# Attention output projection by seven block products for six of its eight column blocks, with the modulation loads and decay constants moved a stage later

## The chip, the cores and the metric

The kernel runs on one core of a Trainium2 chip. The metric is the device time of one execution in microseconds, as the median of several runs. One profiled execution gives the trace; its times are in microseconds from the start of its span.

## The reference

One layer of a hybrid model: 640 tokens (128 of context, 512 latent) with 1024 channels go through an attention branch and a retention branch, whose outputs are projected, gated and added. Cut to what the change touches:

```
z = h @ w_in                                   # q, k, v, rq, rk, rv, rg, ga, gr are split from z
m = jax.nn.silu(cond) @ w_mod + b_mod          # split in 6: sh1, sc1, g1, sh2, sc2, g2
ya = attend_blocks(q, k_all, v_all)
yr, s_f, s_b = retention_branch(rq, rk, rv, rg, ret_pos, dec_f, dec_b, s0_f, s0_b)
y = jax.nn.sigmoid(ga) * (ya @ w_att_o) + jax.nn.sigmoid(gr) * (yr.astype(h.dtype) @ w_ret_o)
...
lg_f = jax.nn.log_sigmoid(dec_f.astype(jnp.float32))
```

The change is about `ya @ w_att_o`, a product of 640 x 1024 by 1024 x 1024, the w_mod products of sc2, sh2, g1 and g2, and the constants made from `dec_f` and `dec_b`.

## The kernel before

Every float32 factor is held as a rounded high part and a low part, and a product is three matmuls, high by high, high by low and low by high. The two halves of the 640 tokens (HALF is 320) are the moving side of a matmul of 128x320; a column block c of a weight is 128 of the 1024 output columns, and k runs over 8 blocks of 128 rows.

The projection is the stage of the PSUM pool `mm3` (five banks) and starts behind attention. `split` (L646/L647) makes high parts on ACT and low parts on DVE of the eight row blocks of the attention output `q4` (tiles `f0.s.3` and `f0.s.4` in the profile), into `ya.u1` and `ya.u2`. Then for each column block c, `load_w` brings two columns' weights and splits them (high part L145 on ACT, low part L150 on DVE, tiles `wh`), `b_col` (L195 to L197) issues 24 matmuls for each half, and `ya_ev` (L793) gates each bank on DVE with `tha[c]` (tiles `f1.s`); L795 spills it on POOL's queue. After each half step a generator, `mod_rest`, is advanced by one: it loads 2 MB of w_mod into a single buffer on SP's queue (L249), waits six steps, issues 64 small matmuls for it (L257) and some follow-up work (L260, L265). In this stage it does four loads (sc2, sh2). `decay_consts` (L580 to L601) makes the decay constants from two small loads; `decay_tables` (L813 to L817) uses them two groups later. A scheduler orders the instructions of each engine by the data they need.

Next come three groups, RK, RQ and RV, by `a_group` (L157 to L159, matmuls of 128x512); each runs in ten steps of twelve matmuls and loads two raw weight tiles of 1 MB. There `mod_rest` is advanced once a step and does the other four loads (g1, g2).

Much later the same kind of projection, `yr @ w_ret_o`, is done by a seven-product scheme (`ret_unit`). For two columns and both halves of the tokens, a pair p, the 2x2 block product is made from seven block products of four k blocks each, twelve matmuls, instead of eight. Its factors need sums: four sums of quarters of the activation (`ret_sums`, L1017 to L1029, each with a high part on ACT and a low part on DVE) and four sums of weight quarters for each pair (`wsum`, L1063). `prep` makes the two parts of one product's weights (L1073, L1082, or L1079 and L1080 through a DMA that accumulates). `prod` issues the matmuls (L1109, L1111, L1112) and the evictions: products 1, 6, 7, 4 add up in one bank and are copied out between (L1114, L1118, L1122, L1126), 5 and 3 share one (L1116, L1129), 2 has its own (L1120). The order of the products is 1, 5, 6, 2, 3, 7, 4, where 4 is held back by two places. A pump keeps up to eight `wh` tiles prepared. Under `tc.manual_schedule` PE, DVE and ACT issue in the order in which the code is written.

## Time and profile before

| what | value |
|---|---|
| median of 3 runs | 1179.63 us (1178.53 to 1179.68) |
| profiled execution | 1177.66 us |
| its span | 1175.9 us |
| mean granted TensorE clock | 0.996 |
| PE busy | 1146.9 us (98%) |
| DVE, ACT, POOL busy | 772.9, 589.7, 182.9 us |
| projection (262.4 to 328.3) | 65.9 us |

PE, DVE, ACT and POOL are TensorE, VectorE, ScalarE and GpSimd; PEld is the loading of weights into PE, and SP the queue that issues most loads. A row of a timeline gives start, duration, engine, line, operation, the tile that it writes and those that it reads, and in brackets how long the engine was idle before and for whom. In a windows row the columns are the stretch, its length, busy time and count for PE, PEld, DVE, ACT and POOL, the granted clock, the DMA share and GB/s.

### The profile page before, as it was taken

What the parts mean: (1) busy time and instruction counts of PE and PEld (TensorE: products, weight loads), DVE (VectorE), ACT (ScalarE), POOL (GpSimd) and SP (SyncE); (2) the same over time, 40 slices, a digit from 0 to 9 for tenths busy, and PEclk for the clock granted to TensorE, in tenths of its full rate; (3) what the DMA queues carried; (4) which work ended last, traced back from release to release, by engine and by line L of the source; (5) the groups of instructions that cost most, each with busy time, mean ns of one, the idle gap of its engine ahead of it and who ended that gap; (6) DMA issues with size and microseconds to landing.
All of it is one profiled execution on the core that took longest, in us unless ns stands there. A gap on an engine that the chain in (4) does not pass through costs nothing.

```text
span 1175.9 us, 18380 instructions
## 1 busy us (share of the span) xinstructions
PE 1146.9 (98%) x7269; PEld 1031.2 (88%) x7269; DVE 772.9 (66%) x1432; ACT 589.7 (50%) x1077; POOL 182.9 (16%) x194
## 2 busy tenths in 40 slices
PE   5999999999999999999999999999999999999995
PEld 4788899999988888888999988999899999899994
DVE  4566977665233536453847739969767588588887
ACT  4355656552132324442445526667657466565463
POOL 0042200000012100033002123002112111121013
PEclk9999999999999999999999999999999999999998
DMA  8742111115754521111117976435666656566553
GB/s 282 254 146 72 37 36 37 37 35 215 260 181 171 172 84 59 37 37 36 54 55 141 275 107 199 108 84 129 145 135 137 148 127 163 126 124 151 129 123 111
DMA packets 135878, 145.84 MB, mean 124 GB/s; under 512 B 26592, under 2 KB 101424, under 8 KB 135792
## 3 DMA queue, kind: packets, MB, share of 16 engines
q1 hardware_dynamic: 106880, 113.60, 29.9%
q0 software_dynamic: 28912, 31.07, 16.5%
q8 instruction: 57, 0.93, 0.3%
q14 instruction: 29, 0.24, 0.1%
HBM read 112.94 MB, written 8.65 MB: 103 GB/s over the span
## 4 chain that ended last, share of the span: by engine, by line
PE 90%; DVE 5%; ACT 2%; issue 1%; POOL 1%; DMA 0%; SPq 0%; DVEq 0%; ACTq 0%; POOLq 0%
POOL f0.s.5_3532 L950 0%; DMA xin.u1.1_108<-in_x_sample 0%; DVE gt.gt0.5_7309 L1380 0%; PE mm3.mm.72_6290 L1109 0%; DVE acts.u2.2_97 L415 0%; PE mm1.mm.11_300 L159 0%; PE mm7.mm.42_9455 L1553 0%; PE mm7.mm.30_8723 L1551 0%; PE mm7.mm.63_10822 L1551 0%; PE mm7.mm.54_10187 L1551 0%; PE mm7.mm.21_8240 L1551 0%; PE mm7.mm.57_10456 L1551 0%; PE mm7.mm.45_9704 L1551 0%; PE mm7.mm.42_9455 L1551 0%; PE mm7.mm.63_10822 L1554 0%
## 5 line engine op out<-in xcount | busy, mean ns | idle before, releaser
L795 POOL DMA_DIRECT2D spill.u2.2_2893<-f1.s.1_1165 x1 | 0.6, 586 | 130.1 <-DVE mod.u4.4_2852 L586 130.1
L1565 DVE TENSOR_TENSOR t7.u4.4_6978<-t7.u4.4_6978,const.u1.1_70 128x322 f32<-128x322 f32 x10 | 5.0, 496 | 11.8 <-ACT const.u1.1_70 L1564 11.8
L1080 POOL DMA_DIRECT2D weights.wh.164_5980<-weights.raw.156_5913 x1 | 1.3, 1347 | 69.5 <-DVE f1.s.9_5324 L1120 69.5
L888 DVE SCALAR_TENSOR_TENSOR ret2.u1.1_4329<-ret2.u1.1_4329,const.u13.13_93 64x128 f32<-64x128 f32 x24 | 6.8, 336 | 6.6 <-ACT ret2.u1.1_4329 L881 6.5
L890 DVE SCALAR_TENSOR_TENSOR ret2.u1.1_4329<-ret2.u1.1_4329,const.u13.13_93 64x128 f32<-64x128 f32 x24 | 6.6, 383 | 4.8 <-ACT ret2.u1.1_4329 L883 4.8
L841 DVE TENSOR_TENSOR ret.u5.5_3535<-ret.u5.5_3535,ret.u1.1_3528 128x512 f32<-128x512 f32 x5 | 3.5, 692 | 9.4 <-POOL ret.r2k.8_3713 L839 3.3
L1476 POOL TENSOR_TENSOR x1.u1.1_6484<-x1.u1.1_6484,weights.raw.422_11041 128x512 f32<-128x512 f32 x5 | 7.9, 1594 | 10.2 <-ACT x1.tm.112_11054 L1449 7.4
L841 DVE TENSOR_TENSOR ret.u4.4_3534<-ret.u4.4_3534,ret.u1.1_3528 128x512 f32<-128x512 f32 x5 | 3.5, 692 | 9.0 <-POOL ret.r2k.11_3893 L839 4.7
L565 POOL TENSOR_TENSOR p1.u1.1_609<-p1.u3.3_613,p1q.u1.1_603 128x512 f32<-128x512 f32 x1 | 1.3, 1307 | 44.8 <-DMA p1.u4.4_615<-in_cache_k 44.8
L150 DVE TENSOR_TENSOR weights.wh.108_4359<-weights.raw.106_4356,weights.wh.107_4358 128x1024 fp32r<-128x1024 f32 x1 | 1.2, 1225 | 10.3 <-ACT weights.wh.107_4358 L145 10.3
L412 ACT CAST acts.u1.1_96<-f0.s.2_110 128x640 fp32r<-128x640 f32 x4 | 2.9, 728 | 10.1 <-DVE f0.s.2_110 L410 10.1
L374 PE MATMUL mm1.mm.1_167<-const.u1.1_70,xin.u1.1_108 128*128 128x128 f32 x4 | 1.1, 435 | 7.0 <-DVE xin.u1.1_108 L365 7.0
L412 ACT CAST acts.u1.1_96<-f0.s.1_109 128x640 fp32r<-128x640 f32 x4 | 2.9, 726 | 9.8 <-DVE f0.s.1_109 L410 9.8
L145 ACT CAST weights.wh.112_4514<-weights.raw.111_4512 128x1024 fp32r<-128x1024 f32 x1 | 1.1, 1050 | 13.3 <-PE mm3.mm.36_4227 L158 13.3
L877 POOL DMA_DIRECT2D out_new_state_ret_fwd<-ret.r2k.25_4352 x1 | 0.7, 664 | 43.8 <-ACT ret.r2k.25_4352 L876 43.8
L260 DVE COPY mod2.wr.9_4319<-aux3.aux.15_4286 128x128 f32<-128x128 f32 x1 | 0.3, 290 | 10.9 <-PE aux3.aux.15_4286 L257 10.9
L950 POOL TENSOR_TENSOR f0.s.5_3532<-f0.s.5_3532,ret2.ny20.11_4911 128x512 f32<-128x512 f32 x5 | 6.0, 1237 | 9.1 <-DVE ret2.ny20.11_4911 L220 9.1
L534 ACT ACTIVATE f0.s.3_715<-f0.s.3_715,p1q.ny20.11_883 128x128 f32<-128x128 f32 x20 | 6.0, 388 | 2.5 <-DVE p1q.ny20.11_883 L218 2.5
L374 PEld LDWEIGHTS mm1.mm.1_167<-const.u1.1_70,xin.u1.1_108 128*128 128x128 f32 x4 | 0.7, 217 | 7.2 <-DVE xin.u1.1_108 L365 7.2
L145 ACT CAST weights.wh.67_3366<-weights.raw.66_3364 128x1024 fp32r<-128x1024 f32 x1 | 1.0, 1045 | 11.5 <-PE mm3.mm.8_3145 L196 11.5
L145 ACT CAST weights.wh.77_3621<-weights.raw.76_3619 128x1024 fp32r<-128x1024 f32 x1 | 1.0, 1045 | 11.5 <-PE mm3.mm.16_3458 L196 11.5
L145 ACT CAST weights.wh.72_3546<-weights.raw.71_3544 128x1024 fp32r<-128x1024 f32 x1 | 1.0, 1045 | 11.4 <-PE mm3.mm.12_3302 L196 11.4
(6929 smaller groups left out, 4936.2 us busy)
## 6 DMA issues: line engine op xcount, KB each, us to landing
spill.u1.1_2892<-x1.u1.1_6484 POOLq DMA_DIRECT2D x5, 512.0 KB, 3.9
xin.u1.1_108<-in_x_sample SPq DMA_DIRECT2D x4, 512.0 KB
p0.u5.5_125<-in_w_mod SPq DMA_DIRECT2D x2, 1024.0 KB
p0.u6.6_131<-in_w_mod SPq DMA_DIRECT2D x2, 1024.0 KB
p0.u7.7_134<-in_w_mod SPq DMA_DIRECT2D x2, 1024.0 KB
mod.wm.6_2920<-in_w_mod SPq DMA_DIRECT2D x1, 2048.0 KB
mod.wm.8_3073<-in_w_mod SPq DMA_DIRECT2D x1, 2048.0 KB
mod.wm.10_3230<-in_w_mod SPq DMA_DIRECT2D x1, 2048.0 KB
```

The costliest lines, as they stand in the source:

```text
L145: nc.scalar.copy(hi, rv)
L374: nc.tensor.transpose(xps[t, g][:, j * P:(j + 1) * P], xin[:, t, k * P:(k + 1) * P], ident)
L412: nc.scalar.copy(hT[0][:, k, :], xk)
L534: nc.scalar.activation(x[:, j], x[:, j], AF.Copy, scale=rstd[:, j:j + 1])
L565: nc.gpsimd.tensor_mul(ct, r2[:, :, 0, :], gqk[:, i:i + 1, :].to_broadcast([P, 4, P]))
L841: V.tensor_mul(z, z, r1[:, t, 0:1, :].to_broadcast([P, 8, 64]))
L888: V.scalar_tensor_tensor(Ss[0:64, hh, st + 1, j], Ss[0:64, hh, st, j], cdsel[0:64, h:h + 1], Ss[0:64, hh, st + 1, j], op0=ALU.mult, op1=AL ...
L890: V.scalar_tensor_tensor(Ss[64:128, hh, 2 - st, j], Ss[64:128, hh, 3 - st, j], cdsel[64:128, h:h + 1], Ss[64:128, hh, 2 - st, j], op0=ALU. ...
L950: nc.gpsimd.tensor_mul(ov, ov, rso[:, 4 * t:4 * t + 4].unsqueeze(2).to_broadcast([P, 4, P]))
L1080: nc.gpsimd.dma_start(lo, src, accum_op=ALU.add)
L1476: eng.tensor_mul(x, x, fg[:, c0:c0 + 512])
L1565: V.tensor_sub(u[1][:, hi_u], u[1][:, hi_u], u3[i])
```

## The change

The code of the seven-product scheme is taken out of `ret_unit` and made general (`seven_unit`, `seven_seq`, `seven_pump`, `seven_run`); w_ret_o uses it as it did. The attention projection now has three parts under a manual schedule. `two_cols` does columns 0 and 1 plainly, in four banks: k 0 to 3 of all four, then k 4 to 7, each bank gated at its end by `ya_ev` (L973 in the new file). `att_sums` and the lines behind it make the four sums in place in `q4` (L912, L916, L919, L923), with high parts by L905 and low parts by L908; they are advanced between the banks, ahead of the gates of those banks. Then pairs 1 to 3 (columns 2 to 7) go by seven products, whose casts are L804, low parts L813, weight sums L794, and whose copies out of banks are L826 (product 1), L828 (5), L830 (6), L834 (7) and L838 (4). The pump also prepares the first half of RK's weights. `decay_consts` and its loads move to the groups behind, into RQ's first step, and all eight w_mod loads are done there, with `mod_rest` advanced twice a step.

The core of the diff:

```
-    mp = Pool("mod", side="right")
-    dec = mp([P, 2, 8])
...
-    decay_consts(dec, dtmp)
-
-    ada = mod_rest((("sc", 1, 4096), ("sh", 1, 3072)), mp, aux)
+    lows, later = [], []
...
-    for c in range(KD):
-        if c % 2 == 0:
-            w = load_w(a["w_att_o"][0, :, c * P:(c + 2) * P], 8, 256)
-        cc = slice((c % 2) * P, (c % 2 + 1) * P)
-
-        def ya_ev(hf, ts, ps, c=c):
...
+    def att_sums():
+        s1, s3, s4 = qf[1, 1], qf[1, 0], qf[0, 1]
+        V.tensor_sub(s1, s1, qf[1, 0])
+        hi_sum(1, s1)
+        yield
+        lo_sum(1, s1)
+        V.scalar_tensor_tensor(s1, s1, -1.0, qf[0, 0], op0=ALU.mult, op1=ALU.subtract)
+        hi_sum(2, s1)
+        yield
+        V.tensor_sub(s3, qf[0, 0], s3)
+        hi_sum(3, s3)
+        lo_sum(2, s1)
+        yield
+        V.scalar_tensor_tensor(s4, s1, -1.0, s4, op0=ALU.mult, op1=ALU.subtract)
+        lo_sum(3, s3)
+        yield
+
+    def two_cols(w, act, ev):
+        banks = {}
+        for kh in range(2):
+            for c in range(2):
+                for hf in range(2):
+                    if kh == 0:
+                        banks[c, hf] = mm([P, 512], tag="mm")[:, :HALF]
+                    ps, ts = banks[c, hf], slice(hf * HALF, (hf + 1) * HALF)
+                    for k in range(4 * kh, 4 * kh + 4):
...
+                    yield
+                    if kh:
+                        ev(c, hf, ts, ps)
...
+    units = {p: seven_unit(w_ao[:, 2 * p * P:2 * (p + 1) * P], ar, u_of(p), p == 1, att_fin(p)) for p in range(1, KD // 2)}
+    seq = seven_seq(units)
+    pump = seven_pump(units, seq, [lambda: wrk.append(w_raw(w_in[:512, O_RK:O_RK + 512], 4, 512))],
+                      [(2, lambda h=h: wrk.append(w_split(wrk[0][:, 1024 * h:1024 * (h + 1)], 2, 512))) for h in range(2)])
+    with tc.manual_schedule(engines={ET.PE, ET.DVE, ET.Activation}):
+        def ya_ev(c, hf, ts, ps):
             V.scalar_tensor_tensor(tha[c][:, ts], tha[c][:, ts], 1.0, ps, op0=ALU.add, op1=ALU.mult)
             if hf:
                 nc.gpsimd.dma_start(thd[:, c, :], tha[c])
-        for _ in b_col(w, cc, yaTk, mm, ya_ev):
-            next(ada, None)
-    run(ada)
-    mp.close()
+
+        for n, _ in enumerate(two_cols(w, yaTk, ya_ev)):
+            if n in (0, 1, 3):
+                next(sums)
+            elif n == 2:
+                pump(-1, 1)
+            elif n == 4:
+                pump(-1, 2)
+            elif n == 5:
+                next(sums)
+            elif n == 6:
+                pump(-1, 4)
+        hi_sum(4, qf[0, 1])
+        lo_sum(4, qf[0, 1])
+        ut.append(f0())
+        seven_run(units, seq, pump)
+        wrk.append(load_w(w_in[512:, O_RK:O_RK + 512], 4, 512))
...
-    ada = mod_rest((("g", 0, 2048), ("g", 1, 5120)), mp, aux)
+    dec = mp([P, 2, 8])
+    dtmp = [mp([P, 2, 8]) for _ in range(3)]
...
+    ada = mod_rest((("sc", 1, 4096), ("sh", 1, 3072), ("g", 0, 2048), ("g", 1, 5120)), mp, aux)
...
-        for j, _ in enumerate(a_group(w_in[:, off:off + 512], hTk, mm, ev)):
+        first = None if i else (lambda: [x + y for x, y in zip(*wrk[1:3])], lambda: wrk[3])
+        for j, _ in enumerate(a_group(w_in[:, off:off + 512], hTk, mm, ev, first=first)):
+            if i == 1 and j == 0:
+                decay_consts(dec, dtmp)
+            next(ada, None)
             next(ada, None)
```

The core of the general unit, which is that of `ret_unit` with the factors and the final step passed in:

```
+        def prep(m):
+            if m in (5, 6):
+                low_part()
+            if m in (4, 5, 6):
+                wsum(m)
...
+            nc.scalar.copy(hi, src)
+            ops[m] = (hi, lo)
+            if m == 5:
+                wsum(7)
+            low_part()
+            if m in (2, 3) and not early:
+                nc.scalar.activation(lo, src, AF.Copy, scale=-1.0)
+                nc.gpsimd.dma_start(lo, src, accum_op=ALU.add)
+            else:
+                lows.append(lambda: V.tensor_sub(lo, src, hi.bitcast(F32)))
...
+            if m == 1:
+                nc.scalar.copy(u[0][:, los], ps)
+            elif m == 5:
+                nc.scalar.activation(u[1][:, his], ps, AF.Copy, scale=-1.0)
+            elif m == 6:
+                nc.scalar.activation(u[1][:, los], ps, AF.Copy, scale=-1.0)
```

What stands on DVE at the start of the projection, before (`ya.u2` are the low parts of the activation, `mod` tiles belong to the decay constants, `wh.60` is a weight's low part, `mm3.mm.1` the first bank):

```order
L647 TENSOR_TENSOR ya.u2.2_2829<-f0.s.3_715,ya.u1.1_2828 128x640 x3
L580 TENSOR_SCALAR mod.u2.2_2850<-mod.u1.1_2849 128x16
L647 TENSOR_TENSOR ya.u2.2_2829<-f0.s.3_715,ya.u1.1_2828 128x640
L647 TENSOR_TENSOR ya.u2.2_2829<-f0.s.4_964,ya.u1.1_2828 128x640 x4
L581 TENSOR_TENSOR mod.u2.2_2850<-mod.u2.2_2850,mod.u1.1_2849 128x16
L593 TENSOR_SCALAR const.u11.11_91<-mod.u1.1_2849 128x16
L150 TENSOR_TENSOR weights.wh.60_3057<-weights.raw.56_3050,weights.wh.59_3056 128x1024
L583 TENSOR_SCALAR mod.u3.3_2851<-mod.u2.2_2850 128x16
L793 SCALAR_TENSOR_TENSOR f1.s.1_1165<-f1.s.1_1165,mm3.mm.1_2904 128x320
```

And under the change, at the same place (`ysum` tiles are the parts of the sums, `raw.56` the raw weights of pair 1, `wh.57` and `wh.58` its first two prepared tiles):

```order
L647 TENSOR_TENSOR ya.u2.2_2829<-f0.s.3_715,ya.u1.1_2828 128x640 x4
L647 TENSOR_TENSOR ya.u2.2_2829<-f0.s.4_964,ya.u1.1_2828 128x640 x4
L912 TENSOR_TENSOR f0.s.4_964<-f0.s.4_964,f0.s.3_715 128x4x320
L908 TENSOR_TENSOR ysum.u2.2_2854<-f0.s.4_964,ysum.u1.1_2853 128x1280
L916 SCALAR_TENSOR_TENSOR f0.s.4_964<-f0.s.4_964,f0.s.3_715 128x4x320
L813 TENSOR_TENSOR weights.wh.57_2917<-weights.raw.56_2915,weights.wh.57_2917 128x512
L919 TENSOR_TENSOR f0.s.3_715<-f0.s.3_715 128x4x320
L908 TENSOR_TENSOR ysum.u4.4_2856<-f0.s.4_964,ysum.u3.3_2855 128x1280
L794 TENSOR_TENSOR weights.raw.56_2915<-weights.raw.56_2915 128x4x128 x2
L813 TENSOR_TENSOR weights.wh.58_2949<-weights.raw.56_2915,weights.wh.58_2949 128x512
L973 SCALAR_TENSOR_TENSOR f1.s.1_1165<-f1.s.1_1165,mm3.mm.1_2871 128x320
L923 SCALAR_TENSOR_TENSOR f0.s.4_964<-f0.s.4_964 128x4x320
```

The decay work is gone from between the low parts; behind the last low part three of the four sums, two of their low parts, two weight sums and two weight low parts now stand ahead of the first gate, and before it was one weight's low part and three small operations.

On ACT, behind the first casts of the activation, before (`wh.59`, `wh.62` and `wh.64` are high parts of weights):

```order
L646 CAST ya.u1.1_2828<-f0.s.3_715 128x640
L646 CAST ya.u1.1_2828<-f0.s.4_964 128x640 x4
L145 CAST weights.wh.59_3056<-weights.raw.56_3050 128x1024
L582 ACTIVATE mod.u2.2_2850<-mod.u2.2_2850 128x16
L145 CAST weights.wh.62_3209<-weights.raw.61_3207 128x1024
L597 ACTIVATE const.u13.13_93<-const.u12.12_92 128x8
```

And under the change (`mm3.mm.5` is the bank of product 1 of pair 1, `wh.57` to `wh.60` the weights of its products 1, 5, 6 and 2):

```order
L646 CAST ya.u1.1_2828<-f0.s.4_964 128x640 x4
L905 CAST ysum.u1.1_2853<-f0.s.4_964 128x1280
L905 CAST ysum.u3.3_2855<-f0.s.4_964 128x1280
L804 CAST weights.wh.57_2917<-weights.raw.56_2915 128x512
L905 CAST ysum.u5.5_2857<-f0.s.3_715 128x1280
L804 CAST weights.wh.58_2949<-weights.raw.56_2915 128x512
L804 CAST weights.wh.59_2983<-weights.raw.56_2915 128x512
L804 CAST weights.wh.60_2985<-weights.raw.56_2915 128x512
L905 CAST ya.u1.1_2828<-f0.s.4_964 128x4x320
L826 COPY f0.s.5_3006<-mm3.mm.5_3007 128x320
```

Four casts of sums and four of weights now stand in one row behind the activation's casts, and the first copy of a product's bank stands behind all eight.

More of the change, by code (lines that the diff above doesn't have):

```diff
@@ L773, in hybrid_step, with low_part @@
     yaTk = [[x[:, k] for k in range(KD)] for x in yaT]
[L774 to L781 removed]
+    lows, later = [], []
+    def low_part():
+        while lows:
+            lows.pop(0)()
@@ new lines, in seven_run @@
+    def seven_run(units, seq, pump, between=None):
+        pend = []
+        for n, (p, m) in enumerate(seq):
+            units[p][2](m)
+            pend.extend((n + d, fn) for d, fn in later)
+            later.clear()
+            if between:
+                between(n)
+            pump(n + 1, min(5 + n, 8))
+            for x in [x for x in pend if x[0] <= n]:
+                x[1]()
+                pend.remove(x)
+        for _, fn in sorted(pend, key=lambda x: x[0]):
+            fn()
@@ L1092, in reload, with tl_load @@
+    def tl_load(n):
+        if n == 15:
             for f in range(2):
                 tl.append(f1())
[L1094 to L1129 removed]
@@ L1131, in ret_unit @@
-        return load, prep, prod, reload
-    w_out = a["w_out"][0]
-    later, pend, wo0 = [], [], []
-    units = [ret_unit(p) for p in range(KD // 2)]
-    order = (1, 5, 6, 2, 3, 7, 4)
-    seq, held = [], []
-    for p in range(KD // 2):
-        for m in order[:-1]:
-            seq.append((p, m))
-            held = [(n - 1, y) for n, y in held]
-            if held and held[0][0] == 0:
-                seq.append(held.pop(0)[1])
-        held.append((2, (p, 4)))
-    seq += [y for _, y in held]
@@ L1146, in hybrid_step @@
[L1146 to L1165 removed]
+                nc.sync.dma_start(tl[f], thd[:, KD - 2 + f, :])
@@ L1167, in hybrid_step @@
+    ar = {1: ya[0, 0], 2: ya[0, 1], 4: ya[1, 1], 3: ys[4]}
+    units = {}
+    seq = seven_seq(range(KD // 2))
     wg = load_w(w_in[:, O_GR:O_GR + 2 * P], 8, 256)
```

252 lines of the change are left out of this document (138 added, 114 removed).

## The prediction

> **What bounds the kernel now.** I read the page's busy times first, then the windows around the stage that changes, then the PE timeline and the chain of waits inside it, and last the DVE and ACT timelines of places where the same operations run today. The page's engine row:
>
> ```profile
> PE 1146.9 (98%) x7269; PEld 1031.2 (88%) x7269; DVE 772.9 (66%) x1432; ACT 589.7 (50%) x1077; POOL 182.9 (16%) x194
> ```
>
> PE is busy 98% of a span of 1175.9 us (the profiled execution took 1177.66 us, 1.97 below the median of 1179.63). The windows view gives the stage before's projection fills and the one after it; the columns are length, busy time of PE, PEld, DVE, ACT and POOL with counts, granted clock, DMA share, GB/s:
>
> ```profile
> 262.40:328.30 65.90, 65.90 (x651) 64.10 (x650) 28.84 (x73) 13.35 (x20) 3.85 (x7) 1.00 0.63 228
> 328.30:430.00 101.70, 101.70 (x619) 82.76 (x622) 39.03 (x72) 29.02 (x52) 17.59 (x21) 1.00 0.47 160
> ```
>
> PE is busy 65.90 of 65.90 us in the projection, and 101.70 of 101.70 behind it, while DVE has 28.84 and ACT 13.35 us of work there. So a matmul removed is its full time gained, and any wait that PE gets is its full time lost. How little PE loses today is seen at the start of the stage, in its timeline:
>
> ```profile
> 262.75 0.31 PE L195 MATMUL mm3.mm.3_2962<-ya.u1.1_2828,weights.wh.52_2896 128*128 128x320 f32 x1
> 263.03 0.41 PE L196 MATMUL mm3.mm.1_2904<-ya.u2.2_2829,weights.wh.52_2896 128*128 128x320 f32 x1
> ```
>
> Before's scheduler puts matmuls of three banks in turn, so that the first correction (L196), which needs the first low half, starts 0.28 us after the matmul ahead of it. That 0.13 us beyond the pitch (0.147, next) is all I see lost there.
>
> **What is removed.** The matmul count falls from 8 columns x 2 halves x 8 k x 3 = 384 to 96 for two plain columns and 3 x 7 x 12 = 252 for six columns by seven products: 36 fewer. The pitch comes from the w_ret_o stage, which runs the same products with the same shape; its first two products on the PE timeline, twelve matmuls apart:
>
> ```profile
> 613.15 0.31 PE L1109 MATMUL mm3.mm.63_5899<-yr.u1.1_5318,weights.wh.152_5832 128*128 128x320 f32 x1
> ...
> 614.91 0.31 PE L1109 MATMUL mm3.mm.64_5921<-f0.s.7_5528,weights.wh.153_5836 128*128 128x320 f32 x1
> ```
>
> 1.76 us for twelve is 0.1467 us each, and 36 of them are **-5.28 us**. The Trainium skill, page "TensorE: Matmul & The Clock Gate", section "Back-to-back issue gap", gives N/2.4 GHz plus about 2.5 ns for a warm matmul, which would be 135.8 ns for 320 columns and 4.89 us for the 36; the rows here show 146.7, so the trace decides, and the difference is 0.39 us. In w_ret_o the scheme costs PE almost nothing beside its matmuls, as the waits of PE there show (total, times, longest):
>
> ```profile
> PE mm3.mm.66_6024 L1109 <- ACT f1.s.12_5327 L1118: 0.2, 1, 0.2
> ```
>
> One wait of 0.2 us in 28 products. That speaks for the change. But there the sums of the activation were made stages earlier, under other matmuls, and weights were prepared four tiles ahead. Here the activation is ready only as the stage begins, and PE has 96 plain matmuls, 14.1 us, to cover all preparation.
>
> **What is added ahead of the products.** For the sums the rows are those of w_ret_o's own sums, DVE and then ACT, 128x1280:
>
> ```profile
> 592.37 1.49 DVE L1023 TENSOR_TENSOR rt.u1.1_5323<-rt.u1.1_5323,yr.u2.2_5319 128x1280 f32<-128x1280 f32 x1
> 595.25 1.49 DVE L1029 TENSOR_TENSOR yr.u2.2_5319<-rt.u1.1_5323,yr.u1.1_5318 128x1280 fp32r<-128x1280 f32 x1 [1.38 <-ACT yr.u1.1_5318 L1028]
> ```
>
> ```profile
> 593.96 1.26 ACT L1028 CAST yr.u1.1_5318<-rt.u1.1_5323 128x1280 fp32r<-128x1280 f32 x1 [1.28 <-DVE rt.u1.1_5323 L1023]
> ```
>
> A sum or a low part is 1.49 us of DVE, a high part 1.26 us of ACT, and a low part begins 0.03 to 0.06 us behind its high part (593.96 + 1.26 = 595.22, then 595.25). Preparing a weight tile (128x512), on DVE a low part (L1082) and a sum (L1063), on ACT negation, cast and eviction in a row:
>
> ```profile
> 621.50 0.69 DVE L1082 TENSOR_TENSOR weights.wh.162_5958<-weights.raw.156_5913,weights.wh.162_5958 128x512 fp32r<-128x512 f32 x1
> 622.22 0.69 DVE L1063 TENSOR_TENSOR weights.raw.156_5913<-weights.raw.156_5913 128x512 f32<-128x512 f32 x1
> ```
>
> ```profile
> 625.09 0.63 ACT L1079 ACTIVATE weights.wh.165_5984<-weights.raw.156_5913 128x512 fp32r<-128x512 f32 x1
> 625.63 0.60 ACT L1073 CAST weights.wh.166_6001<-weights.raw.156_5913 128x512 fp32r<-128x512 f32 x1
> 626.13 0.42 ACT L1122 COPY f1.s.9_5324<-mm3.mm.63_5899 128x320 f32<-128x320 f32 x1
> ```
>
> 0.69 us each on DVE, 0.62 us on ACT (0.52 from start to start when queued), 0.42 for an eviction. A plain column's gate on DVE is the row of before's own eviction:
>
> ```profile
> 269.50 0.48 DVE L793 SCALAR_TENSOR_TENSOR f1.s.1_1165<-f1.s.1_1165,mm3.mm.1_2904 128x320 f32<-128x320 f32 x1
> ```
>
> Twelve sum operations are four sums and four low parts on DVE, 8 x 1.49 = 11.9 us, and four casts on ACT, 5.0 us. They can't start before the low halves of the activation, the last work of DVE that the stage opens with:
>
> ```profile
> 262.15 2.29 DVE L647 TENSOR_TENSOR ya.u2.2_2829<-f0.s.3_715,ya.u1.1_2828 128x640 fp32r<-128x640 f32 x3
> ...
> 264.44 0.82 DVE L647 TENSOR_TENSOR ya.u2.2_2829<-f0.s.3_715,ya.u1.1_2828 128x640 fp32r<-128x640 f32 x1
> 265.18 3.02 DVE L647 TENSOR_TENSOR ya.u2.2_2829<-f0.s.4_964,ya.u1.1_2828 128x640 fp32r<-128x640 f32 x4
> ```
>
> The eighth low half ends at 265.18 + 3.02 = 268.20.
>
> **The walk.** Under the change PE, DVE and ACT go strictly in the written order, so I walked the three queues by hand with these durations, each operation starting when its queue and its inputs allow (0.03 us behind the same engine, 0.06 us over from another, 0.10 to PE). On before's time axis:
>
> a) The first bank now takes k 0 to 3 at once, with nothing of another bank between. The fourth low half ends at 264.44 + 0.82 = 265.26, so its twelve matmuls, which could end at 264.21, end at 265.70: **1.49** late. The other seven groups and product 1 of pair 1 follow without a wait to 279.79.
>
> b) DVE: sum 1 at 268.3, its cast on ACT to 271.1, its low part to 272.7, sum 2 to 274.2, then a wait for ACT (cast of sum 2, then cast of weight tile 1) to 276.1, low part of tile 1, sum 3 and low part 2 to 279.7, two weight sums and a low part to 281.7, and only then the gate of the first plain bank, to 282.2. Product 5 needs that bank (five banks, four of them plain, one product 1's). It starts at 282.27 instead of 279.79: **2.48**.
>
> c) DVE next has sum 4, low part 3 and a second gate, and the weight sum of product 6 ends at 286.0. ACT waits for this sum with the cast of tile 6, then casts tile 2 and the high part of sum 4 (1.26), and behind these stands the copy of product 1 out of its bank, 288.3 to 288.8. Product 6 adds into that bank, so it starts at 288.86 and not at 284.03: **4.83**. This is the largest term: a copy that could run at 280 stands behind a queue that waits for DVE.
>
> d) Later a bank's copy stands behind weight casts that wait for their DVE sums: product 4 of pair 1 waits 1.32 (copy of 7), product 6 of pair 2 0.68 (copy of 1), product 7 of pair 2 0.54 (copy of 6): **2.54**. A last wait of 0.75 ahead of the final product lies behind three RK matmuls that the order puts there, and costs nothing.
>
> The waits are 1.49 + 2.48 + 4.83 + 2.54 = 11.34 us. Their bounds: with every hand-over free the walk gives 10.2, with 0.12 us for each 12.5; if the 1280-wide operations take 0.75 of their rows, 7.8. For d) zero (as in w_ret_o) to twice as much.
>
> **What is moved.** All eight w_mod loads of 2 MB now run under RK, RQ and RV, twice as often. The 64 matmuls of each load, and the issue of each load on SP's queue (L249):
>
> ```profile
> L257 PE MATMUL aux3.aux.9_3665<-mod2.wm.2_3569,mod2.s128.1_3566 x64: 272/273/297, 347.8 to 349.5; 128*32 128x128 f32 x64
> ...
> L257 PE MATMUL aux3.aux.11_3835<-mod2.wm.4_3736,mod2.s128.1_3566 x64: 272/273/297, 372.3 to 374.0; 128*32 128x128 f32 x64
> ```
>
> ```profile
> L249 SPq DMA_DIRECT2D mod2.wm.2_3569<-in_w_mod x1: 1068/1068/1068, 326.7 to 326.7; - x1
> L249 SPq DMA_DIRECT2D mod2.wm.4_3736<-in_w_mod x1: 367/367/367, 349.8 to 349.8; - x1
> ```
>
> Two sets start 24.5 us apart, of which 1.88 are the set itself, so a load has half of 22.6, **11.3 us**, from the release of its only buffer to its next set. When loads landed is read from the transfer rate by windows:
>
> ```profile
> 338.00:339.00 1.00, 1.00 (x6) 0.82 (x5) 0.00 (x0) 0.00 (x0) 0.00 (x0) 1.00 0.60 225
> 339.00:340.00 1.00, 1.00 (x6) 0.83 (x5) 0.00 (x0) 0.00 (x0) 0.00 (x0) 1.00 0.14 53
> 357.00:358.00 1.00, 1.00 (x6) 0.83 (x5) 0.31 (x1) 0.76 (x1) 0.66 (x1) 1.00 0.05 16
> ```
>
> The one issued at 349.8 had landed by 357.1 (7.3 us); the one at 326.7, beside the rope table and a 1-MB weight load, by 339.3 (12.6 us). The SP queue keeps the weight loads between, and before's projection ran 228 GB/s without a PE wait, while the stage behind it (160 GB/s over 101.7 us, 16.3 MB) rises by 8.4 MB over 7.5 us more, to some 226. I take 0.3 us in all, for the first load, and keep 0 and 1.3 per load as ends. The decay constants are small operations off PE's path and needed only by the tables in RV; their two loads stand on SP ahead of the first w_mod load. I put them at nothing: DVE and ACT have 60% idle there. The RK weights' first half is prepared under the products; nothing of it is late in the walk.
>
> **The sum.** -5.28 + 11.34 - 0.13 (before's own loss) + 0.3 = **+6.23**, own time 1177.66 + 6.23 = 1183.89, and beside a median that lay 1.97 higher, 1185.9.
>
> **The rivals.** Differences under 0.2%, 2.4 us, can't be told from no change by this measurement. The forecast has a chance of 0.60.
>
> *The later waits don't come* (0.15). PE, once late, gives DVE and ACT time, and w_ret_o showed one wait only; against it, the same queues here start without four tiles in hand. Waits 8.80: +3.69, median 1183.3.
>
> *The clock falls in the 4.8 us pause* (0.10 as a case of its own). The windows at the end, after the last matmul at 1164.02:
>
> ```profile
> 1164.00:1167.00 3.00, 0.02 (x1) 0.00 (x0) 2.86 (x13) 2.53 (x8) 0.53 (x1) 1.00 0.01 3
> 1167.00:1168.00 1.00, 0.00 (x0) 0.00 (x0) 0.96 (x4) 1.00 (x3) 0.54 (x1) 0.82 0.39 150
> 1168.00:1169.00 1.00, 0.00 (x0) 0.00 (x0) 0.96 (x3) 1.00 (x2) 0.00 (x0) 0.50 1.02 385
> ```
>
> A clock of 0.82 in the second of these means that full rate ended near 1167.64, after 3.6 us of no matmul. At the kernel's start, after 6.98 us idle, groups of four transposes:
>
> ```profile
> 13.13 1.12 PE L374 MATMUL mm1.mm.1_167<-const.u1.1_70,xin.u1.1_108 128*128 128x128 f32 x4 [6.98 <-DVE xin.u1.1_108 L365]
> ...
> 17.40 0.60 PE L374 MATMUL mm1.mm.6_213<-const.u1.1_70,xin.u1.1_108 128*128 128x128 f32 x4
> 17.84 0.60 PE L374 MATMUL mm1.mm.7_225<-const.u1.1_70,xin.u1.1_108 128*128 128x128 f32 x4
> ```
>
> Five groups took 4.27 us where one takes 0.44 later: 2.07 us lost. In the walk product 6 at half rate just uses up the waits of d), and the end stays where it was. Without these waits it adds to the rival above: +5.8. With both it is +8.3, median 1187.9. The Trainium skill, the page named above, section "What's actually happening", puts the fall to 1.2 GHz at an idle window of about 3.4 us; the trace's 3.6 agrees.
>
> *Each w_mod load comes late* (0.09). For it: 12.6 us in one case against 11.3. Against: 7.3 in the other. 1.3 x 8 = 10.4 at most, half of it the likely size: +11.1, median 1190.8.
>
> *The sums are cheaper than their rows, and the change wins* (0.06). In place it is one mechanism: the 1280-wide operations of c) and b). At half their price the walk's first two waits in b) and c) shrink to 0.17, all waits to 4.1, and with d) gone too to 1.66: -3.45, median 1176.2. Against it: every row of such an operation shows 1.49, in place or not. It decides the sign when all waits are under 5.1 us, and is a gain that can be told when they are under 2.7. Total waits between 2.7 and 7.5 would be no difference.
>
> **Range and chances.** The range takes in the walk at 0.75 of the sums' price (waits 7.8, +2.7, median 1182.3) with half of d) gone (1181.0), and on the other side d) doubled with the clock's 2.07 (+10.8, 1190.5). I give 1181.0 to 1190.5. Faster by over 0.2%: 0.05, most of the last rival. Within: 0.07, the rest of it and the low end of the first. Slower: 0.88.
>
> **What would show it.** In the profile after: PE's waits in the stage on L973 (about 2.5 us, product 5) and L826 (about 4.8, product 6), a first bank stretched by 1.5 us, small ones on L826, L830 and L834; granted clock below 1.00 behind the long wait; DVE's 1280-wide rows at 1.49; sets of L257 some 13.1 us apart from 335 on without waits on DMA. I am wrong if PE stays full through the stage, if the copy of product 1 (L826) comes near 280, or if the lost time is found behind the stage.

## The result and the profile after

The change makes the kernel slower: 1185.45 us (1185.35 to 1186.38, 4 runs) against 1179.08 us before (4 runs), a ratio of 1.0056 with a 95% interval of 1.0044 to 1.0068. That is 6.4 us. The profiled execution of the changed kernel has a span of 1183.8 us, 7.9 above that of before; 1.0 of this lies ahead of the stage, in the start of the kernel, which no edit touches. From the first matmul of the projection to the first product of the w_ret_o stage it is 357.14 us (263.48 to 620.62 on the PE timeline) against 350.70 (262.45 to 613.15): 6.44 us more, the same as the medians say.

The page's engine row: PE has 36 instructions fewer and is 97% busy in place of 98%, and DVE 24.7 us more.

```profile
PE 1146.4 (97%) x7233; PEld 1027.2 (87%) x7233; DVE 797.6 (67%) x1464; ACT 607.1 (51%) x1115; POOL 188.5 (16%) x198
```

The longest waits of PE in the projection and the three groups behind it; before's list of waits was empty for the projection (total, times, longest):

```profile
PE mm3.mm.5_3007 L821 <- ACT f0.s.5_3006 L826: 4.4, 1, 4.4
PE mm3.mm.6_3029 L821 <- DVE f1.s.1_1165 L973: 2.0, 1, 2.0
PE aux3.aux.10_4011 L265 <- DVE mod2.wr.15_3980 L260: 0.3, 1, 0.3
PE mm3.mm.8_3132 L821 <- ACT f0.s.5_3006 L826: 0.3, 1, 0.3
PE aux3.aux.1_3473 L257 <- DMA mod2.wm.6_3435<-in_w_mod: 0.3, 1, 0.3
```

The two large ones are those at product 6 of pair 1, for L826, and at product 5, for L973. The PE timeline has both, and how long product 6 took (first rows of products 5, 6 and 2):

```profile
282.88 0.39 PE L821 MATMUL mm3.mm.6_3029<-ysum.u1.1_2853,weights.wh.58_2949 128*128 128x320 f32 x1 [1.99 <-DVE f1.s.1_1165 L973]
...
289.25 0.63 PE L821 MATMUL mm3.mm.5_3007<-ysum.u3.3_2855,weights.wh.59_2983 128*128 128x320 f32 x1 [4.37 <-ACT f0.s.5_3006 L826]
...
292.42 0.31 PE L821 MATMUL mm3.mm.7_3074<-ya.u1.1_2828,weights.wh.60_2985 128*128 128x320 f32 x1
```

Product 6 starts 6.37 us behind product 5, where its turn would be 1.76, and itself takes 292.42 - 289.25 = 3.17 us and not 1.76. The granted clock says why, in the column ahead of DMA share and GB/s:

```profile
288.00:289.00 1.00, 0.00 (x0) 0.00 (x0) 1.00 (x3) 1.00 (x2) 0.00 (x0) 0.89 0.21 82
289.00:290.00 1.00, 0.76 (x3) 0.76 (x4) 1.00 (x2) 1.00 (x3) 0.39 (x1) 0.50 0.00 0
...
292.00:293.00 1.00, 1.00 (x8) 1.00 (x7) 0.52 (x1) 0.45 (x1) 0.00 (x0) 0.91 0.03 10
```

It fell in the pause, at about 288.8, and was at half rate until 292.2. Behind that PE hardly waits: 0.47 us at product 6 of pair 2 and 0.36 at product 7, from start to start. What ACT did ahead of product 6's release, and DVE ahead of that:

```profile
286.57 0.62 ACT L804 CAST weights.wh.59_2983<-weights.raw.56_2915 128x512 fp32r<-128x512 f32 x1 [4.96 <-DVE weights.raw.56_2915 L794]
287.10 0.61 ACT L804 CAST weights.wh.60_2985<-weights.raw.56_2915 128x512 fp32r<-128x512 f32 x1
287.62 1.25 ACT L905 CAST ya.u1.1_2828<-f0.s.4_964 128x1280 fp32r<-128x1280 f32 x1
288.78 0.41 ACT L826 COPY f0.s.5_3006<-mm3.mm.5_3007 128x320 f32<-128x320 f32 x1
```

```profile
282.65 1.48 DVE L923 SCALAR_TENSOR_TENSOR f0.s.4_964<-f0.s.4_964 128x1280 f32<-128x1280 f32 x1
284.05 1.49 DVE L908 TENSOR_TENSOR ysum.u6.6_2858<-f0.s.3_715,ysum.u5.5_2857 128x1280 fp32r<-128x1280 f32 x1
285.46 0.48 DVE L973 SCALAR_TENSOR_TENSOR f1.s.1_1165<-f1.s.1_1165,mm3.mm.2_2886 128x320 f32<-128x320 f32 x1
285.85 0.69 DVE L794 TENSOR_TENSOR weights.raw.56_2915<-weights.raw.56_2915 128x512 f32<-128x512 f32 x1
```

ACT waited 4.96 us for the weight sum of product 6 (L794, 285.85), which stands on DVE behind sum 4 (L923), low part 3 (L908) and a gate (L973); then come two casts, the high part of sum 4 and only then the copy. This is the chain of the prediction's point c), step by step: once the 1.03 us by which the stage starts later are taken off, each step comes 0.1 to 0.6 us ahead of where the walk has it.

### The profile page after: what moved, and what is told of

It reads as the page before. It is cut to its first block, busy times and chain, and to the rows that moved or that the text cites. A ratio compares the mean times of both kernels' runs of the same rounds, so it can differ in the third digit from the quotient of the medians.

```text
span 1183.8 us, 18404 instructions
## 1 busy us (share of the span) xinstructions
PE 1146.4 (97%) x7233; PEld 1027.2 (87%) x7233; DVE 797.6 (67%) x1464; ACT 607.1 (51%) x1115; POOL 188.5 (16%) x198
## 4 chain that ended last, share of the span: by engine, by line
PE 57%; DVE 4%; ACT 3%; issue 2%; DMA 1%; POOL 1%; DVEq 0%; ACTq 0%; POOLq 0%; SPq 0%
DMA weights.wh.419_10834<-weights.raw.406_10564 0%; DMA weights.raw.423_10893<-in_w_down 0%; POOL f0.s.6_3402 L1152 0%; DVE gt.gt0.5_7362 L1489 0%; PE mm3.mm.69_6341 L821 0%; PE mm7.mm.42_9508 L1660 0%; PE mm7.mm.30_8776 L1660 0%; PE mm7.mm.54_10240 L1660 0%; PE mm7.mm.33_9025 L1660 0%; PE mm7.mm.45_9757 L1660 0%; PE mm7.mm.21_8293 L1660 0%; PE mm7.mm.57_10509 L1660 0%; PE mm7.mm.54_10240 L1663 0%; PE mm7.mm.30_8776 L1663 0%; PE mm7.mm.39_9376 L1660 0%
## 5 line engine op out<-in xcount | busy, mean ns | idle before, releaser
L260 DVE COPY mod2.wr.21_4372<-aux3.aux.15_4339 128x128 f32<-128x128 f32 x1 | 0.3, 292 | 10.9 <-PE aux3.aux.15_4339 L257 10.9
L1552 DVE TENSOR_TENSOR x1.u1.1_6537<-x1.u1.1_6537,gate.u1.1_6508 128x512 f32<-128x512 f32 x10 | 6.8, 688 | 0.0
L1009 ACT ACTIVATE ret.u2.2_3400<-const.u1.1_70,const.u11.11_91 128x128 f32<-128x128 f32 x8 | 3.1, 388 | 7.1 <-DVE const.u11.11_91 L594 7.1
```

The costliest lines, as they stand in the source:

```text
L1009: nc.scalar.activation(dmat[:, h, :], cst[:, C_RF:C_RF + P], AF.Exp, scale=lg[:, 0, h:h + 1])
L1552: V.tensor_mul(x1[:, t, gs], x1[:, t, gs], gb[:, t == 0, gs])
```

## The experiments

The measure beside the time is the stage's length, from the first matmul of the projection to the first of the last product, from the PE timeline. It has 336 matmuls at 0.1467 and 0.70 us of three RK matmuls, 49.99 us without a wait. In the change it is 324.09 - 263.48 = 60.61. The first four runs shared a chip, then the next three, then the last three, each with runs of the kernel before.

**The moves alone.** The kernel before with the w_mod loads and the decay constants moved:

```
-        for _ in b_col(w, cc, yaTk, mm, ya_ev):
-            next(ada, None)
-    run(ada)
+        run(b_col(w, cc, yaTk, mm, ya_ev))
...
+            if i == 1 and j == 0:
+                decay_consts(dec, dtmp)
+            next(ada, None)
             next(ada, None)
```

> The kernel before, with only the moves of the change: all eight w_mod loads and the decay constants under RK, RQ and RV, the projection as it was. Theory A (the loss is made by the waits of the projection's products, the moves cost little): the trace of the change shows two pauses of about 0.5 us at the moved sets, so about 1180 us, within 0.2% of the kernel before. Theory B (the moves are the price, through loads that land late): 1183 us or more, with PE waiting for w_mod loads several times.

Measured: 1180.37 us, ratio 1.001 (1.0001 to 1.0018). From the projection's first matmul to w_ret_o it is 351.76 us, 1.06 more than before. PE waits twice behind the stage:

```profile
PE aux3.aux.11_4012 L257 <- DMA mod2.wm.16_3949<-in_w_mod: 0.4, 1, 0.4
PE aux3.aux.10_3951 L265 <- DVE mod2.wr.15_3920 L260: 0.3, 1, 0.3
```

So the moves cost about 1.1 us, one late load and one wait for the copy of a finished set (L260); no load is late again and again. The other 5.3 of the 6.4 us are the products.

**Without the sums.** The activation's sums and their parts are left out, and products 5, 6, 7 and 3 use plain quarters:

```
-    ysum = {m: [ysp([P, 4, HALF], F32R) for _ in range(2)] for m in (1, 2, 3)}
-    ysum[4] = yq[1, 0]
+    ysum = {1: yq[1, 1], 2: yq[0, 0], 3: yq[0, 1], 4: yq[1, 0]}
...
-        hi_sum(4, qf[0, 1])
-        lo_sum(4, qf[0, 1])
```

> The change without the four sums of the activation and their high and low parts: the products that need a sum take a plain quarter instead, so the output is not the reference's. Theory A (the sums fill DVE and ACT and hold PE up): the pauses of product 5 and product 6 go, about 1.5 us at the first bank and about 1 us later remain, so -5.3 + 2.0 + 1.0 - 0.1 = -2.4 against the kernel before, about 1176.7 us, and no fall of the clock. Rival (weight preparation alone is too slow for the products): pauses of 2 us and more remain, and the time is 1180 us or more.

Measured: 1176.58 us, ratio 0.998 (0.9972 to 0.9989), within 0.2 us of what theory A gave. The stage is 51.95 us long. The longest wait of PE in it:

```profile
PE mm3.mm.1_2862 L936 <- DVE ya.u2.2_2829 L647: 0.3, 1, 0.3
```

The weights alone keep up with PE; the pauses belong to the sums, and without them the seven products win 2.6 us.

**Copies and gates first.**

```
-                    yield
                     if kh:
                         ev(c, hf, ts, ps)
+                    yield
...
             elif n == 5:
+                pump(-1, 4)
+            elif n == 6:
                 next(sums)
-            elif n == 6:
-                pump(-1, 4)
-        hi_sum(4, qf[0, 1])
-        lo_sum(4, qf[0, 1])
+        def sum4(n):
+            if n == 0:
+                hi_sum(4, qf[0, 1])
+                lo_sum(4, qf[0, 1])
```

> The change with the evictions put ahead: each gate ahead of the sums and weights of its step, the preparation of products 6 and 2 ahead of the fourth sum, and that sum's parts behind the copy of product 1. Nothing is left out. Theory A1 (the prediction's words: copies stand behind sums in the queue, and this place is the price): the pause of product 6 falls from 4.4 us to about 1, so 1180.5 to 1182.5 us. Theory A2 (DVE and ACT have a fixed row of work with hand-overs up to product 7 of pair 2, and PE must wait for its end wherever the copies stand): pauses only move to products 3, 7 and 4 of pair 1, and the time stays within 0.8 us of the change, 1184.7 to 1186.2 us.

Measured: 1188.24 us, ratio 1.0075 (1.0062 to 1.0089), and a stage of 62.03 us, 1.42 longer than the change's. Both theories missed: the pause of product 6 did not fall. The waits of PE, then the two rows of DVE and ACT that end it:

```profile
PE mm3.mm.5_3005 L821 <- ACT f0.s.5_3004 L826: 5.0, 1, 5.0
PE mm3.mm.6_3029 L821 <- ACT weights.wh.58_2950 L804: 1.2, 1, 1.2
```

```profile
287.71 1.48 DVE L908 TENSOR_TENSOR ysum.u6.6_2858<-f0.s.3_715,ysum.u5.5_2857 128x1280 fp32r<-128x1280 f32 x1
```

```profile
289.31 0.42 ACT L826 COPY f0.s.5_3004<-mm3.mm.5_3005 128x320 f32<-128x320 f32 x1 [4.12 <-DVE ysum.u6.6_2858 L908]
```

The copy now finds ACT's queue empty: ACT is idle for 4.12 us before it, and it is released by the low part of sum 3 on DVE. It writes `f0.s.5`. The pool `f0` has two buffers (`bufs=2`), both held by the attention output, and the low part of sum 3 is the last to read the first of them (`f0.s.3`). So the copy had a second wait that neither the prediction nor these theories had; in the change it is hidden, since the low part ends at 285.5 and the copy starts at 288.78.

**The plain columns in turns by k.** The twelve matmuls of one k go to all four banks before the next k:

```
+        for k in range(4):
+            for c, hf in banks:
+                ps, ts = banks[c, hf], slice(hf * HALF, (hf + 1) * HALF)
...
+            yield
```

> The change with the first four k blocks of the two plain columns issued k by k over the four banks, not bank by bank, so that PE does not wait for the low halves at the start. Theory A2 (the row of DVE and ACT sets when product 5 can go, and PE is early anyway): the 1.4 us at the first bank become about 0.5 and come back at product 5, 1184.9 to 1186.0 us. Rival (each pause is a loss of its own): 1 us less, about 1184.4 us.

Measured: 1186.96 us, ratio 1.0071 (1.0058 to 1.0084); this interval and the change's (1.0044 to 1.0068) overlap, though the time lies 1 us above what theory A2 gave. The first bank's wait fell from 1.40 to 0.52 us (start of the second bank in turn 263.77, 0.96 behind the first with 0.44 of matmuls), but the stage is 60.58 us long, against 60.61 without the edit. The waits:

```profile
PE mm3.mm.5_3007 L821 <- ACT f0.s.5_3006 L826: 3.1, 1, 3.1
PE mm3.mm.6_3029 L821 <- DVE f1.s.1_1165 L979: 2.9, 1, 2.9
```

Product 5 waits 2.9 in place of 2.0. What PE gains ahead of a pause, it waits longer in the pause, as theory A2 has it. (The clock fell twice in this execution, which made product 5 itself longer and the pause behind it shorter.)

**Sum 3 early.** The run with the copies first, with the low part of sum 3 right behind that of sum 2:

```
         lo_sum(2, s1)
+        lo_sum(3, s3)
         yield
         V.scalar_tensor_tensor(s4, s1, -1.0, s4, op0=ALU.mult, op1=ALU.subtract)
-        lo_sum(3, s3)
         yield
```

> The order of the run with the copies first, with one more step: the low part of the third sum stands right behind that of the second, ahead of the gates. In the run with the copies first the copy of product 1 was released by this low part, because it writes into the buffer of the first half of the activation. Theory C (that buffer held the copy): the pause of product 6 falls from 5.0 to about 1.1 us. Theory A2 (the row of work on DVE and ACT decides the end): the stage ends no earlier for that; walked by hand the pauses are 3.5 at product 5, 1.1 at 6, and 2.0, 1.3 and 1.6 at products 3, 7 and 4 of pair 1, the end 1.1 us later than in the change, about 1186.5 us. Rival A1 (the copy's place is the price): about 4 us faster than the run with the copies first, 1183 to 1184.5 us.

Measured: 1187.7 us, ratio 1.0076 (1.0062 to 1.0089), stage 61.63 us. The waits of PE (product 5; 4 and 7 of pair 1; 3 of pair 1):

```profile
PE mm3.mm.6_3029 L821 <- ACT weights.wh.58_2951 L804: 2.6, 1, 2.6
PE mm3.mm.5_3005 L821 <- ACT f0.s.5_3004 L834: 1.4, 1, 1.4
PE mm3.mm.5_3005 L821 <- ACT f0.s.5_3004 L830: 1.0, 1, 1.0
PE mm3.mm.6_3029 L821 <- ACT f0.s.5_3004 L828: 0.9, 1, 0.9
```

Now nothing but casts of weights stands ahead of the copy, and it runs as they end:

```profile
285.82 0.41 ACT L826 COPY f0.s.5_3004<-mm3.mm.5_3005 128x320 f32<-128x320 f32 x1
```

That is 22.77 us behind the stage's start, and 25.56 with the copies first, which shows that the buffer held the copy. PE has no pause left at product 6, but not by this alone: product 5 ran at half rate for most of its 3.56 us, 1.8 more than at full rate, and that covers the rest of the pause. And the stage is 0.4 us shorter than with the copies first, not 4: the time comes back at products 5, 3, 7 and 4. It ends 1.0 us later than the change's, where the walk had 1.1. The place of the copy was not the price.

**Another order of the same operations.** DVE, ACT and PE get the change's operations from one written list, of which the start is

```
load1 load2 K000 K001 K010 K011 K100 K101 K110 K111 K200 w1.3 K201 K210 w1.1 K211 lw1.1 K300 K301 s1
K310 K311 C00 ws1.5 s3 w1.5 hs1 C01 lw1.5 w2.1 ev00 hs3 ls1 C10 s2 C11 ls3 hs2 p1.1 ws1.6 s4 w1.6
p1.5 w1.2 w2.2 ls2 e1.1 hs4 lw1.6 p1.6 e1.5 ev01 lw1.2 ls4 p1.2 ws1.7 lw1.3 w1.7 p1.3 ev10 n2.2
```

where K and C are plain blocks, s, hs and ls a sum and its high and low part, ws, w and lw the same of a weight (pair and product), n a negation, ev a gate, p a product and e its copy.

> All operations of the change, in another written order on DVE and ACT, found by moving single operations in the hand walk (with the waits for buffers in it): the first two weight casts ahead of the sums, sums 1 and 3 before the first low part, weight operations in the hand-overs between DVE and ACT, low parts of weights later than their casts, copies as soon as their product ends; the plain columns take turns by k. The walk has 0.5 us of waits at the first matmuls and 1.1 us behind them, and ends 9.3 us before the change. Theory A2 (hand-overs and order make the pauses, not the amount of work): 1176 to 1177.5 us, faster than the kernel before. Rival (12 us of sums on DVE can't be hidden behind 14 us of plain matmuls at all): 1183 us or more, with pauses of several us at products 5 to 7 of pair 1.

Measured: 1176.98 us, ratio 0.9983 (0.9974 to 0.9992): faster than the kernel before, and 8.5 us faster than the change. The stage is 51.66 us long, 8.95 shorter than the change's; the walk had 9.3. The longest waits of PE in it, and DVE's row through the first sums:

```profile
PE mm3.mm.9_3129 L1062 <- ACT f0.s.5_3030 L1070: 0.5, 1, 0.5
PE mm3.mm.1_2875 L989 <- DVE ya.u2.2_2829 L647: 0.3, 1, 0.3
```

```profile
268.39 1.49 DVE L1020 TENSOR_TENSOR f0.s.4_964<-f0.s.4_964,f0.s.3_715 128x1280 f32<-128x1280 f32 x1
269.80 0.68 DVE L1045 TENSOR_TENSOR weights.raw.56_2871<-weights.raw.56_2871 128x512 f32<-128x512 f32 x1
270.41 1.48 DVE L1024 TENSOR_TENSOR f0.s.3_715<-f0.s.3_715 128x1280 f32<-128x1280 f32 x1
271.81 0.68 DVE L1051 TENSOR_TENSOR weights.wh.60_2947<-weights.raw.56_2871,weights.wh.60_2947 128x512 fp32r<-128x512 f32 x1
```

DVE has no idle time ahead of any of these: weight work (L1045, L1051) stands between the activation's sums (L1020, L1024), where it would wait for ACT. In the change it does wait there:

```profile
272.00 1.49 DVE L908 TENSOR_TENSOR ysum.u2.2_2854<-f0.s.4_964,ysum.u1.1_2853 128x1280 fp32r<-128x1280 f32 x1 [1.33 <-ACT ysum.u1.1_2853 L905]
276.86 0.69 DVE L813 TENSOR_TENSOR weights.wh.57_2917<-weights.raw.56_2915,weights.wh.57_2917 128x512 fp32r<-128x512 f32 x1 [1.85 <-ACT weights.wh.57_2917 L804]
```

Nothing was left out (DVE and ACT have 1464 and 1115 instructions in both), so 12 us of sums on DVE can be hidden; what the change loses is in the order. Which of the many moves brought how much, this run does not tell.

**Keeping PE busy in the pause.** Idle matmuls between products 5 and 6:

```
+        def warm(n):
+            if n == 1:
+                ps = aux([P, 512], tag="aux")
+                for _ in range(26):
+                    nc.tensor.matmul(ps[:, :P], ident, ident, start=True, stop=True)
+        seven_run(units, seq, pump, warm)
```

> The change with 26 idle matmuls of 128x128 into a bank that nobody reads, on PE between products 5 and 6 of pair 1, about 2.9 us of its 4.4 us pause, so that the clock doesn't fall. They add nothing to DVE and ACT. Theory A2 (PE is early again right behind the pause, so time at half rate is taken from later waits): product 6 takes 1.76 us in place of 3.17, waits of about 1.3 us come up at product 4 of pair 1 and behind it, and the end stays within 0.4 us of the change, 1185 to 1186.2 us. Rival (the 1.41 us at half rate are a loss of their own): 1184.1 us, with no new waits.

Measured: 1188.17 us, ratio 1.0074 (1.0062 to 1.0087), stage 61.02 us. Neither theory was tested as meant, because I had mis-sized the idle matmuls:

```profile
285.23 6.74 PE L996 MATMUL aux3.aux.1_3043<-const.u1.1_70 128*128 128x128 f32 x52
291.73 0.39 PE L821 MATMUL mm3.mm.5_3007<-ysum.u3.3_2855,weights.wh.59_2983 128*128 128x320 f32 x1
```

They took 6.5 us, and product 6 came 28.54 us behind the stage's start, 2.77 later than in the change. What it does show is that these 2.77 us, with product 6 then at full rate (1.86 us), cost the stage only 0.41. The rest of the longer time lies behind the stage: PE waits 1.1 us at L265 for L260 and 1.3 us at L275 for a copy of ACT, and neither wait is as long in the change's profile.

**Keeping PE busy, shorter,** with 11 of them:

> The run with the idle matmuls again, with 11 in place of 26: they took 0.235 us each there, not 0.11, and moved product 6 itself by 2.8 us; 11 take 2.6 us of the 4.4 us pause. Theory A2: product 6 starts when it does in the change, 25.8 us after the stage's start, runs at full rate in 1.76 us, waits of 0.5 to 1.3 us come up at products 4 of pair 1 and 6 and 7 of pair 2, and the stage ends within 0.4 us of the change (60.6 us from its start to the last product). Rival (half rate is a loss of its own): the stage ends 1.4 us earlier, 59.2 us.

Measured: 1186.19 us, ratio 1.0059 (1.0046 to 1.0071), stage 60.57 us. The waits of PE on products and the clock behind the pause:

```profile
PE mm3.mm.5_3007 L821 <- ACT f0.s.5_3006 L826: 1.9, 1, 1.9
PE mm3.mm.5_3007 L821 <- ACT f0.s.5_3006 L834: 0.9, 1, 0.9
```

```profile
288.00:291.00 3.00, 2.65 (x18) 2.66 (x19) 3.00 (x6) 1.67 (x4) 0.55 (x1) 1.00 0.28 109
```

Product 6 starts 25.75 us behind the stage's start and takes 1.86 us at full rate. Product 4 of pair 1 now waits for L834, and from start to start 1.11 us are lost there, 0.68 at product 6 of pair 2 and 0.34 at product 7; the stage ends where the change's does, 60.57 against 60.61.

**The change again,** on that chip:

> The change itself on this chip, to set the two others against: 1185 to 1186.5 us, pauses of 2.0 and 4.4 us at products 5 and 6.

Measured: 1185.95 us, ratio 1.006 (1.0048 to 1.0073), stage 60.74 us. The longest wait of PE, and the clock behind the pause as above:

```profile
PE mm3.mm.5_3007 L821 <- ACT f0.s.5_3006 L826: 4.4, 1, 4.4
```

```profile
288.00:291.00 3.00, 2.47 (x9) 2.48 (x10) 3.00 (x5) 1.86 (x5) 0.55 (x1) 0.50 0.30 110
```

In this execution the clock stayed at half rate until 294.06; products 6 and 2 took 3.36 and 2.77 us, 2.61 us more than at full rate, and from there PE did not wait at all. Three executions in which products 6 and 2 took 0.1, 1.4 and 2.6 us more than at full rate thus end their stage within 0.17 us of each other. In the first two DVE and ACT set that end, and PE waits for them; in the third the half rate has just used up these waits.

**Filling the hand-overs,** by a few moves in the change's own code:

```
+        pump(-1, 1)
         for n, _ in enumerate(two_cols(w, yaTk, ya_ev)):
...
         hi_sum(1, s1)
+        V.tensor_sub(s3, qf[0, 0], s3)
+        hi_sum(3, s3)
+        lo_sum(1, s1)
         yield
-        lo_sum(1, s1)
         V.scalar_tensor_tensor(s1, s1, -1.0, qf[0, 0], op0=ALU.mult, op1=ALU.subtract)
         hi_sum(2, s1)
-        yield
-        V.tensor_sub(s3, qf[0, 0], s3)
-        hi_sum(3, s3)
+        lo_sum(3, s3)
         lo_sum(2, s1)
         yield
```

Gates and the fourth sum's parts stand as in the run with the copies first, and product 5's weights ahead of sum 2.

> The change with few steps moved and nothing left out: the weight cast and low part of product 1 ahead of the sums, sum 3 right behind sum 1, so that DVE works while ACT casts sum 1, the weights of product 5 ahead of sum 2, gates ahead of the work of their step, the parts of sum 4 behind the copy of product 1. The work of DVE and ACT is the same; what goes are hand-overs in which DVE waited for ACT. Theory A2: the pauses of products 5 and 6 fall to 1.5 us together, the clock doesn't fall, smaller waits of 1 to 2 us stay at products 3, 7 and 4 of pair 1, and the stage ends 3 to 3.5 us earlier than in the change, about 1182 us. Rival (only the total of work counts): no change, 1185 us or more. Rival (the first pauses are all the price): 1179 us.

Measured: 1182.31 us, ratio 1.0029 (1.0018 to 1.0041), 3.6 us less than the change beside it, stage 57.27 us, 3.34 less than the first profile of the change. The waits (4, 3 and 7 of pair 1, 6 of pair 2):

```profile
PE mm3.mm.5_3005 L821 <- ACT f0.s.5_3004 L834: 1.4, 1, 1.4
PE mm3.mm.6_3029 L821 <- ACT f0.s.5_3004 L828: 1.1, 1, 1.1
PE mm3.mm.5_3005 L821 <- ACT f0.s.5_3004 L830: 1.0, 1, 1.0
PE mm3.mm.8_3132 L821 <- ACT f0.s.5_3004 L826: 0.4, 1, 0.4
```

The pauses of products 5 and 6 are gone, and smaller ones of products further back have come up, as expected, 3.9 us in all. The operations of DVE and ACT are those of the change. The two waits of DVE for ACT shown above, 1.33 and 1.85 us, are gone, and the clock did not fall.

## Why the prediction was right

**The sum.** It had +6.23 us; the medians gave +6.37 and the trace +6.44 over the span that the change touches. That it came within 0.2 us is in part luck: the waits of the stage were forecast as 11.34 and are 60.61 - 49.99 = 10.62, 0.72 less, and the moves were forecast as 0.3 and cost 1.06, 0.76 more. The two misses cancel.

**36 matmuls, -5.28.** Right: plain banks and products follow each other 1.76 us apart in every run, and the stage without sums, 51.95 us, lies 2.0 above what 336 matmuls and the RK ones make at 0.1467.

**a) to c).** Forecast 1.49, 2.48 and 4.83; measured from start to start 266.64 - 263.48 - 1.76 = 1.40, 282.88 - 280.72 = 2.16 and 289.25 - 284.64 = 4.61. They are 0.63 us too long together.

**d), and the clock.** Here the text took the likelier case without the clock's fall, 2.54 us of later waits. The clock did fall. 1.41 us of half rate and 0.83 of waits stand in the trace, 2.24 together, and 2.61 and none in the second profile. The prediction had this in its rival: product 6 at half rate uses up the waits of d). The shorter run with idle matmuls shows the reverse of it: at full rate the waits of d) come up and the end stays. The 2.07 us that the prediction put on the clock were read from slow transposes at the kernel's start; the granted clock is 1.00 in every window of before from 13 to 18 us, so these rows don't show its price. In this stage it was 1.41 and 2.61 us.

**The moves.** 0.3 was too little: 1.06 us in the run of the moves alone, and 0.46 and 0.51 us at two sets in the changed kernel's PE timeline (336.34 to 336.80, 395.23 to 395.74). The first is the load forecast to be late; the second, a wait of L265 for the copy of the set (L260), was not foreseen.

**Where the reason was wrong.** The sentence on c) that a copy which could run at 280 stands behind a queue is true of the order and false as the cause of the price. The copy could not have run before the low part of sum 3, at 285.5, because of the buffer, which the walk lacked; and with this removed as well, the run with sum 3 early has its copy 2.8 us sooner than with the copies first and still a stage 1.0 us longer than the change's. The price is how late DVE and ACT come through the sums and the weights of the first seven to eleven products, their hand-overs included: 8.95 us of it went when the same operations stood in another order.

**The rivals.** Late loads at every set did not come. The sums cost what their rows said (1.48 to 1.49). That the later waits don't come is what the second profile shows, with the clock in their place.

What stays open: outside of what the edits touch, from w_ret_o's first product to the last matmul, the profiles took 550.6 (before) to 553.4 us (copies first). Part of it is one wait of PE at L275 for a copy of ACT (L277): it is 0.4 to 1.3 us long in the moves alone, copies first, turns by k, the longer idle matmuls and the change again, and the other profiles don't have it. The granted clock is 1.00 there in all of them. The rest has no known cause. This is one reason why medians of the variants differ from each other by up to 2.3 us more than their stages do.

## What to carry to other kernels

When a step that PE must wait for is made by two engines that hand work to each other, walk all three queues in their written order, and take the result as a length of the row on the slower ones and not as a list of separate pauses: a pause removed by moving one copy, by starting PE earlier or by keeping its clock up comes back further on. Then look for idle time at the hand-overs and put other work of the same engines there. And put the release of buffers into the walk; here a copy waited for an array that had nothing to do with it but its place.

## What the runs showed of the hardware

The stretches at half rate have one length, or twice that. From the windows of 1 us, they were 3.40 us in the changed kernel, 3.40 and 3.42 with turns by k, 3.40 with sum 3 early, 3.42 in the longer run with idle matmuls, and 6.84 and 6.82 with the copies first and in the change again. They begin at times that lie whole steps of 3.41 us apart. With turns by k the clock fell twice:

```profile
282.00:283.00 1.00, 0.80 (x4) 0.83 (x5) 1.00 (x2) 0.00 (x0) 0.00 (x0) 0.79 0.00 0
289.00:290.00 1.00, 1.00 (x7) 1.00 (x7) 1.00 (x2) 0.89 (x3) 0.48 (x1) 0.70 0.06 16
```

A granted clock of 0.79 in 1 us with a fall to half means 0.58 us at full rate, so it fell at 282.58, and again at 289.40, which is 6.82 later, two steps. With sum 3 early it fell at 23.90 and 283.32, and in the longer run with idle matmuls at 24.02 and 283.44: 259.42 us both times, 76 steps of 3.413. So the steps go on through an execution, whatever PE does.

A fall came after as little as 2.0 us without a matmul, in the longer run with idle matmuls (last matmul of product 1, first of product 5; then the clock):

```profile
280.29 0.31 PE L824 MATMUL mm3.mm.5_3007<-ya.u1.1_2828,weights.wh.57_2917 128*128 128x320 f32 x1
282.59 0.39 PE L821 MATMUL mm3.mm.6_3029<-ysum.u1.1_2853,weights.wh.58_2949 128*128 128x320 f32 x1 [1.99 <-DVE f1.s.1_1165 L973]
```

```profile
283.00:284.00 1.00, 1.00 (x7) 1.00 (x7) 1.00 (x2) 0.00 (x0) 0.00 (x0) 0.72 0.07 16
284.00:286.00 2.00, 2.00 (x10) 2.00 (x9) 2.00 (x3) 0.00 (x0) 0.06 (x1) 0.50 0.00 0
```

Full rate ended at about 283.44, after PE had come back for 0.85 us. In the changed kernel the same pause, 2.0 us, left the clock alone. Both fit the steps: the one from 280.03 to 283.44 has the whole 2.0 us of the pause in it, while in the changed kernel, counted back from 288.78, an edge at 281.95 cuts the pause into 1.1 us and 0.9 us, and the step behind the edge has 0.5 us of the next pause too. The most that a step had without a fall was 1.7 us, in the change again (280.47 to 282.17, with the edge counted back from its fall at 287.30). The two stretches of double length have 1.1 and 1.2 us without a matmul in their first step, and the single one of the changed kernel has 0.5. The Trainium skill, page "TensorE: Matmul & The Clock Gate", section "What's actually happening", has a free-running window of about 3.4 us, which agrees with the lengths, and the fall after a window that is idle; the trace has a fall after one that was idle for 2.0 of 3.41 us.

An idle matmul of 128x128 in float32 took 0.25 us (6.5 us for 26, each with two rows in the trace, the first 1.6 us at half rate), and 0.24 at full rate in the shorter run (2.6 us for 11), about twice the 0.11 that the expectation took from the transposes at the kernel's start.
